# Planning the instruction order of a two-layer hybrid decoder with the framework's other timing model

## The chip, the core and the metric

The kernel runs on one core of one Trainium2 chip. The core has five engines that each work through a list of instructions of their own, in order: TensorE (PE, matrix products), VectorE (DVE), ScalarE (ACT), GpSimd (POOL) and SyncE (SP, which here only starts DMA transfers). They meet through semaphores. The metric is the device time of one execution in microseconds (us).

## What is computed

A prompt of 256 tokens and 8 samples of 4 tokens (T = 288 columns in all) go through two layers with shared weights. Layer 0 mixes tokens by retention (4 heads, chunked, rotary positions), layer 1 by a gated DeltaNet (GDN: short causal convolution, per-head decay, chunked delta rule). Each is followed by a gated ConvFFN with D_FF = 2816. Ahead of every sub-layer stands an RMS norm whose shift, scale and gate come from the conditioning vector c ("modulation"):

```python
for l in range(DEPTH):
    mod = cs @ p['w_ada'][l] + p['b_ada'][l]
    sh1, sc1, g1, sh2, sc2, g2 = jnp.split(mod, 6, axis=-1)
    h = ada_rmsnorm(x, p['norm_mix'][l], sh1, sc1)
    out, S = retention_mixer(h, ...) if l % N_MIXERS == 0 else gdn_mixer(h, ...)
    x = x + g1[:, None, :] * out
    h = ada_rmsnorm(x, p['norm_ffn'][l], sh2, sc2)
    out, buf = conv_ffn(h, s_fconv[l], p['w_ffn_up'][l], p['w_ffn_dw'][l], p['b_ffn_dw'][l], p['w_ffn_down'][l])
    x = x + g2[:, None, :] * out
y = ada_rmsnorm(x, p['norm_final'], shf, scf)
```

Outputs are y for both groups and the states that the mixers and convolutions leave. All is float32.

## The kernel before

The activations stay on the core; the weights, some 234 MB with the states, are streamed once. `plan_weights` lists them in the order of use as tiles of 128 x 1024 floats (512 KB), and `load` (L400) starts one DMA for each on SP's queue, into slots `raw` or `more` as these come free. A weight tile is split in two parts that a fast matmul can take, `whi` (a copy by ACT, L414) and `wlo` (the rest, by DVE, L415), and `product` (L533) makes 24 matmuls of it, each 128x128 by 128x288: eight each for `whi` with the high part of the activations (`hh`), `whi` with the low part (`hl`), and `wlo` with `hh`. The tiles' names tell the product: `pe`, `p`, `pv`, `pg` in retention, `fg` and `fv` up and `down` down in the ConvFFN, `gk`, `gv`, `gz` and `down` in GDN.

The modulation weights come as such tiles too. `ada_step` makes four matmuls of one, `adaP` (L453); eight tiles make a chunk, which ACT evicts (`adaev`) and `adaT` (L462) transposes. They wait for nothing but their DMA, and the source spreads them over the program, partly (`FILL`, `FILLS`, `ada_due`) at the places where a norm is made: ahead of its statistics `st_...` (L558), between these and their broadcast `rb_...` (L564, with DVE's inverse root between the two), and behind.

GDN works in four groups of four value heads. A group's work is a chain of small steps over PE, DVE and ACT: gates (`pg`), decays (`pd`, L1246), scores (`pa`, L1275; `pq`), an inverse by levels (`uc`, `pe` L1345), the heads' state chain (`pw`, `pn`, `po`), normalisation (DVE's `bigc`, L1618), the state update `gpS` (L1623), `px` (L1641) and `pxs` (L1647), then the gated output `gah` and the product `down`. The samples' states are loaded as tiles `gS` (L1436) and read by `pks` (L1466). `GDN_ORDER` and generators that `tick` steps inside the products (every six matmuls) interleave these chains with the large products in the source.

The order in which each engine gets its instructions is not the source order alone: the framework plans it from the source order and a timing model of its own, and the slots of a pool are given out by it too. `build` opens the pools and runs the stages; `__init__` calls it:

```python
with ExitStack() as ret:
    ...
    hs = self.retention(hs, lambda: self.h_split(1, 3, 4, "ffn0"))
hs = self.ffn(0, hs, 5, lambda: self.h_split(2, 6, 7, "gdn"))
hs = self.gdn(hs, lambda: self.h_split(3, 9, 10, "ffn1"))
self.ffn(1, hs, 11, self.finish)
```

Of the kernel before, what the change touches and what calls it, by code (L numbers as in the profile page):

```python
# [293 lines left out]
class Program:  # L294
    def __init__(self, ctx, tc, A, prm_offs, upto=99):
        self.ctx, self.tc, self.nc, self.A = ctx, tc, tc.nc, A
        self.upto = upto
        self.prm_offs = prm_offs
        self.cst_offs = shape_constants()[0]
        self.build()  # L300

    def pool(self, ctx, name, bufs=1, space=None):
        kw = {"space": space} if space else {}
# [1426 lines left out]
```

## Time and profile before

| what | value |
|---|---|
| median of 3 runs | 1236.14 us (1232.62 to 1408.05) |
| profiled execution, time | 1235.09 us |
| profiled execution, span from the first to the last instruction | 1233.3 us |
| PE busy | 1162.4 us (94%) |
| DVE busy | 877.2 us (71%) |
| ACT busy | 608.4 us (49%) |
| POOL busy | 326.0 us (26%) |
| DMA, mean over the span | 218 GB/s |
| granted TensorE clock, mean | 0.978 |

Busy time is the union of an engine's instructions. The stages follow one another on PE: retention up to about 345 us, the first ConvFFN to about 580, GDN to about 985, the second ConvFFN to about 1220, then the final norm.

### The profile page before, as it was taken

What the parts mean: (1) busy time and instruction counts of PE and PEld (TensorE: products, weight loads), DVE (VectorE), ACT (ScalarE), POOL (GpSimd) and SP (SyncE); (2) the same over time, 40 slices, a digit from 0 to 9 for tenths busy, and PEclk for the clock granted to TensorE, in tenths of its full rate; (3) what the DMA queues carried; (4) which work ended last, traced back from release to release, by engine and by line L of the source; (5) the groups of instructions that cost most, each with busy time, mean ns of one, the idle gap of its engine ahead of it and who ended that gap; (6) DMA issues with size and microseconds to landing.
All of it is one profiled execution on the core that took longest, in us unless ns stands there. A gap on an engine that the chain in (4) does not pass through costs nothing.

```text
span 1233.3 us, 24974 instructions
## 1 busy us (share of the span) xinstructions
PE 1162.4 (94%) x9486; PEld 1045.2 (85%) x9486; DVE 877.2 (71%) x2038; ACT 608.4 (49%) x1258; POOL 326.0 (26%) x504
## 2 busy tenths in 40 slices
PE   6999999999999999999889888988899899999996
PEld 2879788797969999997777777977789699999996
DVE  3657574765766666667769888797965687878785
ACT  2444534344446445543674655745544365555542
POOL 0214142151301221233242124243222212233241
PEclk9999999999999999999989998999999899999997
DMA  9999696866689556556636652534334997878521
GB/s 350 347 335 331 224 338 230 315 239 236 226 298 400 196 161 199 171 181 243 219 84 209 218 165 61 161 129 120 126 109 130 307 358 257 258 238 264 182 76 39
DMA packets 97480, 269.08 MB, mean 218 GB/s; under 512 B 26816, under 2 KB 28832, under 8 KB 97232
## 3 DMA queue, kind: packets, MB, share of 16 engines
q1 hardware_dynamic: 87456, 234.42, 56.6%
q0 software_dynamic: 8032, 29.16, 6.3%
q10 hardware_dynamic: 1872, 3.90, 0.9%
q8 instruction: 75, 1.23, 0.4%
q14 instruction: 45, 0.37, 0.1%
HBM read 236.06 MB, written 31.39 MB: 217 GB/s over the span
## 4 chain that ended last, share of the span: by engine, by line
PE 77%; DVE 13%; ACT 3%; DMA 3%; issue 2%; POOL 1%; ACTq 0%; POOLq 0%; DVEq 0%
PE down L533 17%; PE fg L533 12%; PE fv L533 11%; PE pg L533 4%; PE pv L533 4%; PE adaP L453 4%; PE p L533 3%; PE gv L533 2%; PE gz L533 2%; DVE mp L1319 2%; DVE wlo L415 2%; PE gk L533 2%; PE pO L884 1%; PE pU L903 1%; PE pS L854 1%
## 5 line engine op out<-in xcount | busy, mean ns | idle before, releaser
L415 DVE TENSOR_TENSOR wlo<-more,whi 128x1024 fp32r<-128x1024 f32 x138 | 171.1, 1241 | 80.6 <-ACT whi L414 67.8
L414 ACT CAST whi<-more 128x1024 fp32r<-128x1024 f32 x138 | 144.4, 1048 | 139.6 <-PE down L533 53.3
L414 ACT CAST whi<-raw 128x1024 fp32r<-128x1024 f32 x123 | 128.0, 1044 | 146.3 <-PE down L533 44.1
L415 DVE TENSOR_TENSOR wlo<-raw,whi 128x1024 fp32r<-128x1024 f32 x123 | 154.2, 1256 | 60.6 <-ACT whi L414 36.5
L702 POOL TENSOR_TENSOR x<-x,dt 128x32 f32<-128x32 f32 x159 | 103.1, 649 | 138.9 <-DVE dt L700 137.2
L698 DVE SCALAR_TENSOR_TENSOR x<-down,mod,x 128x256 f32<-128x256 f32 x160 | 76.7, 479 | 52.5 <-PE down L533 51.9
L580 POOL TENSOR_TENSOR fal<-cv,fah 128x288 fp32r<-128x288 f32 x44 | 41.2, 936 | 217.3 <-ACT fah L579 186.3
L533 PE MATMUL down<-fal,whi 128*128 128x288 f32 x352 | 64.5, 295 | 0.0
L533 PE MATMUL down<-fah,whi 128*128 128x288 f32 x352 | 62.2, 294 | 0.0
L533 PE MATMUL down<-fah,wlo 128*128 128x288 f32 x352 | 62.1, 294 | 0.0
L904 DVE SCALAR_TENSOR_TENSOR S<-S,pU 128x512 f32<-128x512 f32 x64 | 42.2, 684 | 24.5 <-PE pU L903 24.4
L533 PE MATMUL fg<-hh_ffn,whi 128*128 128x288 f32 x352 | 58.4, 298 | 0.8 <-ACT hh_ffn L626 0.7
L533 PE MATMUL fv<-hh_ffn,whi 128*128 128x288 f32 x352 | 58.7, 297 | 0.0
L533 PE MATMUL fg<-hh_ffn,wlo 128*128 128x288 f32 x352 | 55.0, 296 | 0.0
L533 PE MATMUL fv<-hh_ffn,wlo 128*128 128x288 f32 x352 | 54.7, 295 | 0.0
L533 PE MATMUL fv<-hl_ffn,whi 128*128 128x288 f32 x352 | 54.2, 295 | 0.0
L533 PEld LDWEIGHTS fg<-hh_ffn,whi 128*128 128x128 f32 x352 | 50.3, 188 | 4.6 <-ACT hh_ffn L632 2.2
L533 PE MATMUL fg<-hl_ffn,whi 128*128 128x288 f32 x352 | 54.0, 295 | 0.0
L533 PEld LDWEIGHTS down<-fal,whi 128*128 128x128 f32 x352 | 52.4, 188 | 0.4 <-issue 0.4
L533 PEld LDWEIGHTS down<-fah,whi 128*128 128x128 f32 x352 | 51.9, 188 | 0.8 <-ACT whi L414 0.8
L533 PEld LDWEIGHTS fv<-hh_ffn,whi 128*128 128x128 f32 x352 | 50.3, 188 | 2.5 <-ACT ftail L934 1.2
L533 PEld LDWEIGHTS down<-fah,wlo 128*128 128x128 f32 x352 | 51.9, 188 | 0.0
(467 smaller groups left out, 2921.3 us busy)
## 6 DMA issues: line engine op xcount, KB each, us to landing
more<-in_wu SPq DMA_DIRECT2D x73, 512.0 KB, 5.2
raw<-in_wada SPq DMA_DIRECT2D x69, 512.0 KB, 4.8
raw<-in_wgi SPq DMA_DIRECT2D x48, 512.0 KB, 3.9
more<-in_wada SPq DMA_DIRECT2D x43, 512.0 KB, 6.3
more<-in_wd SPq DMA_DIRECT2D x36, 512.0 KB, 3.8
S<-in_sr SPq DMA_DIRECT2D x16, 1024.0 KB, 8.5
out_rs<-S POOLq DMA_DIRECT2D x16, 1024.0 KB, 6.9
raw<-in_wri SPq DMA_DIRECT2D x28, 512.0 KB, 4.6
```

The lines of the kernel that those rows point to most:

```text
L414: nc.scalar.copy(hi[:, :c], r)
L415: nc.vector.tensor_tensor(lo[:, :c], r, hi[:, :c].bitcast(F32), ALU.subtract)
L453: nc.tensor.matmul(self.adaP[32 * g : 32 * g + 32, 0:256], lhsT=self.cs[:, k, :], rhs=rv[:, :, g, :], start=(k == 0), stop=(k == KT - 1), ...
L533: self.nc.tensor.matmul(out, lhsT=av[:, k, c0 : c0 + m], rhs=b[:, k, :], start=(k0 == 0 and i == 0), stop=(k1 == kts and i == len(seq) - 1))
L580: (nc.gpsimd if pool_lo else nc.vector).tensor_tensor(lo, src, hi.bitcast(F32), ALU.subtract)
L698: nc.vector.scalar_tensor_tensor(xm[:, :TP], p[:, :TP], g[:, 0:1], xm[:, :TP], ALU.mult, ALU.add)
L702: (nc.vector if gate == 11 and last and m == KT - 1 else nc.gpsimd).tensor_tensor(xv, xv, t, ALU.add)
L854: nc.tensor.matmul(pS, lhsT=kt[:, j, c * P : (c + 1) * P], rhs=vt[:, j, :], start=(j == 0), stop=(j == 1))
L884: nc.tensor.matmul(pO4[32 * g : 32 * g + 32, :], lhsT=qm[:, c, 4 * bb + g, :], rhs=S[bb, c][:, g, :], start=(bb == 0 and c == 0), stop=Fal ...
L903: nc.tensor.matmul(pU, lhsT=kms[g][:, c * P : (c + 1) * P], rhs=vst, start=True, stop=True)
L904: nc.vector.scalar_tensor_tensor(S[bb, c][:, g, :], S[bb, c][:, g, :], gamma4, pU, ALU.mult, ALU.add)
L1319: nc.vector.tensor_tensor(m, Ti[:, 0:k, :].rearrange("p j c -> p c j").unsqueeze(1).to_broadcast([P, w, 8, k]), X[:, 0:k, i:k].rearrange(" ...
```

## The change

The whole program is built inside a block of the framework that plans the order with its other timing model:

```diff
--- before.py
+++ after.py
@@ -297,7 +297,8 @@
         self.upto = upto
         self.prm_offs = prm_offs
         self.cst_offs = shape_constants()[0]
-        self.build()
+        with tc.block(schedule_with_timeline_sim=True), ExitStack() as self.ctx:
+            self.build()
 
     def pool(self, ctx, name, bufs=1, space=None):
         kw = {"space": space} if space else {}
```

The source order stays as it was, and every instruction is there as before; line numbers behind L300 and the numbers in names are one higher. The pools now close inside the block. What differs is the order on each engine, and with it the slots of the pools. The ConvFFN stages keep theirs; the three places below are in the other stages or between them.

First, SP's queue at the start, where tiles of retention weights (`in_wri`) and modulation weights (`in_wada`) are loaded. Before:

```order
L400 DMA raw<-in_wri 128x1024
L400 DMA raw<-in_wada 128x1024 x3
L400 DMA more_149<-in_wada 128x1024
L400 DMA raw<-in_wri 128x1024
L400 DMA more_161<-in_wada 128x1024
L400 DMA raw<-in_wada 128x1024
L400 DMA more_169<-in_wada 128x1024
L400 DMA more_197<-in_wada 128x1024
L400 DMA more_203<-in_wri 128x1024
L400 DMA more_205<-in_wri 128x1024
L400 DMA more_207<-in_wri 128x1024
L400 DMA more_209<-in_wri 128x1024
```

Now:

```order
L401 DMA raw<-in_wri 128x1024
L401 DMA raw<-in_wada 128x1024 x3
L401 DMA more_206<-in_wri 128x1024
L401 DMA more_150<-in_wada 128x1024
L401 DMA more_208<-in_wri 128x1024
L401 DMA more_210<-in_wri 128x1024
L401 DMA more_162<-in_wada 128x1024
L401 DMA more_170<-in_wada 128x1024
L401 DMA more_198<-in_wada 128x1024
L401 DMA more_204<-in_wri 128x1024
L401 DMA raw<-in_wri 128x1024
L401 DMA raw<-in_wada 128x1024 x3
```

The three `more` tiles of `in_wri` from the end of the first list have come forward between the modulation tiles, and the second `raw` tile of `in_wri` has gone from behind one modulation tile (`more_149`) to behind all of these.

Second, PE at the entry of the first ConvFFN: the last modulation matmuls ahead of the norm's statistics `st_ffn`, then its broadcast `rb_ffn`, then the first up products `fg` and `fv`. Before:

```order
L453 MATMUL adaP<-more_3435,c 32x256 x2
L453 MATMUL adaP<-more_3492,c 32x256 x4
L453 MATMUL adaP<-more_3631,c 32x256 x4
L453 MATMUL adaP<-raw,c 32x256 x5
L558 MATMUL st_ffn_3804<-ones,ssum 128x1 x3
L453 MATMUL adaP<-raw,c 32x256 x11
L462 MATMUL adaT<-cst,adaev 128x128 x2
L453 MATMUL adaP<-more_3786,c 32x256 x4
L564 MATMUL rb_ffn_3865<-cst,tr_ffn_3808 128x128 x2
L564 MATMUL rb_ffn_3865<-cst,tr_ffn_3808 128x32
L453 MATMUL adaP<-more_3792,c 32x256 x4
L533 MATMUL fg_3981<-hh_ffn_3769,whi 128x288
```

Now:

```order
L454 MATMUL adaP<-raw,c 32x256 x12
L454 MATMUL adaP<-more_3787,c 32x256 x4
L454 MATMUL adaP<-more_3793,c 32x256 x4
L454 MATMUL adaP<-more_3799,c 32x256 x4
L454 MATMUL adaP<-raw,c 32x256 x4
L559 MATMUL st_ffn_3805<-ones,ssum 128x1 x3
L463 MATMUL adaT<-cst,adaev 128x128 x2
L454 MATMUL adaP<-raw,c 32x256 x12
L565 MATMUL rb_ffn_3866<-cst,tr_ffn_3809 128x128 x2
L565 MATMUL rb_ffn_3866<-cst,tr_ffn_3809 128x32
L454 MATMUL adaP<-more_3856,c 32x256 x4
L534 MATMUL fg_3982<-hh_ffn_3770,whi 128x288 x3
```

Ahead of `st_ffn` there are now 28 matmuls `adaP` in a row where there were 15, behind it fewer, and three k-tiles of `fg` come in one go.

Third, PE at the end of GDN: the last `po` of group 3, its `gpS`, `px` and `pxs`, and the product `down` of its output (with `gah_11546` before, `gah_11547` now). Before:

```order
L1584 MATMUL po_11237<-bigc,gat_9611 128x128
L1586 MATMUL po_11237<-bigc,gat_9611 128x128
L533 MATMUL down<-gal_11050,whi 128x288 x2
L533 MATMUL down<-gah_11049,wlo 128x288 x4
...
L533 MATMUL down<-gal_11050,whi 128x288 x3
L1623 MATMUL gpS_11301<-bigc,kn_9444 128x256 x4
L533 MATMUL down<-gal_11050,whi 128x288
...
L533 MATMUL gz_11504<-hh_gdn,wlo 128x288 x8
L1641 MATMUL px_11530<-cst,bigc 128x128 x4
L1641 MATMUL px_11536<-cst,bigc 128x128 x4
L453 MATMUL adaP<-raw,c 32x256 x8
L1647 MATMUL pxs_11542<-cst,ons_11309 128x128
```

Now:

```order
L1585 MATMUL po_11238<-bigc,gat_9612 128x128
L1587 MATMUL po_11238<-bigc,gat_9612 128x128
L1585 MATMUL po_11238<-bigc,gat_9612 128x128
L1587 MATMUL po_11238<-bigc,gat_9612 128x128
L454 MATMUL adaP<-raw,c 32x256 x8
L1624 MATMUL gpS_11302<-bigc,kn_9445 128x256 x4
L1642 MATMUL px_11531<-cst,bigc 128x128 x4
L454 MATMUL adaP<-raw,c 32x256 x4
L1642 MATMUL px_11537<-cst,bigc 128x128 x4
L1648 MATMUL pxs_11543<-cst,ons_11310 128x128
L534 MATMUL down<-gah_11547,whi 128x288 x4
```

The `down` matmuls of group 2 and the products `gz` of group 3 that stood between `po`, `gpS` and `px` stand further up, ahead of this chain; between `po` and `gpS` there are eight matmuls `adaP` left.

## Rows read from the trace of the kernel before

**Rows 1.** Stages: stretch, length, busy PE, PEld, DVE, ACT, POOL (counts), clock, DMA, GB/s

```profile
0.00:50.00 50.00, 35.88 (x251) 22.37 (x252) 24.18 (x61) 16.29 (x29) 4.49 (x13) 0.97 0.92 354
50.00:345.00 295.00, 294.83 (x2191) 253.30 (x2190) 187.45 (x338) 130.77 (x226) 85.08 (x106) 1.00 0.77 275
345.00:600.00 255.00, 249.84 (x2035) 232.71 (x2036) 166.91 (x360) 121.46 (x219) 58.04 (x77) 1.00 0.69 236
600.00:900.00 300.00, 265.60 (x2456) 234.60 (x2455) 255.01 (x700) 172.95 (x465) 94.27 (x183) 0.95 0.46 140
900.00:990.00 90.00, 84.10 (x735) 74.37 (x734) 57.85 (x140) 40.70 (x86) 20.64 (x35) 0.96 0.62 198
990.00:1220.00 230.00, 229.15 (x1814) 225.10 (x1813) 180.12 (x426) 122.76 (x228) 63.50 (x91) 0.99 0.64 213
```

**Rows 2.** Waits of PE: waiter, releaser, total us, times, longest

```profile
PE pa L1275 <- DVE gat L1282: 6.9, 3, 2.9
...
PE pks L1466 <- DMA gS<-in_sg: 5.9, 6, 2.0
...
PE gpS L1623 <- DVE bigc L1618: 4.5, 3, 2.5
...
PE psy L1480 <- DVE t L1482: 2.3, 2, 2.2
...
PE gk L533 <- DVE gcv L1098: 1.8, 1, 1.8
...
PE pd L1246 <- ACT gat L1254: 1.0, 1, 1.0
...
PE pd L1246 <- POOL decay L1232: 0.8, 1, 0.8
```

**Rows 3.** Timeline of PE, first layer's start: start us, us, engine, line, operation

```profile
31.43 0.69 PE L533 MATMUL pe<-hh_ret,whi 128*128 128x288 f32 x4
31.95 0.69 PE L533 MATMUL pe<-hl_ret,whi 128*128 128x288 f32 x4
```

**Rows 4.** Timeline of SP's queue at the start; page's DMA issues, costliest groups

```profile
14.46 0.33 SPq L400 DMA_DIRECT2D more<-in_wada  x1
...
23.19 0.33 SPq L400 DMA_DIRECT2D raw<-in_wri  x1
...
raw<-in_wri SPq DMA_DIRECT2D x28, 512.0 KB, 4.6
...
L414 ACT CAST whi<-raw 128x1024 fp32r<-128x1024 f32 x123 | 128.0, 1044 | 146.3 <-PE down L533 44.1
```

**Rows 5.** Timeline of PE at the entry of the first ConvFFN

```profile
345.49 0.83 PE L558 MATMUL st_ffn<-ones,ssum 128*128 128x1 f32 x6 [0.56 <-DVE ssum L599]
...
351.81 0.40 PE L533 MATMUL fg<-hh_ffn,whi 128*128 128x288 f32 x1 [0.73 <-ACT hh_ffn L626]
...
353.57 0.64 PE L453 MATMUL adaP<-raw,c 128*32 128x256 f32 x8
```

**Rows 6.** One stretch there, columns as in the first group

```profile
348.00:352.00 4.00, 2.62 (x25) 1.45 (x26) 2.54 (x10) 1.27 (x4) 0.16 (x1) 1.00 1.01 398
```

**Rows 7.** Tile gS: its DMA to landing

```profile
DMA to landing us min/median/max: 3.8/4.6/6.3
```

**Rows 8.** Timeline of PE at the end of the GDN stage

```profile
931.03 0.39 PE L1586 MATMUL po<-bigc,gat 128*128 128x128 f32 x2
...
938.63 1.97 PE L1623 MATMUL gpS<-bigc,kn 128*128 128x256 f32 x8
...
955.48 1.04 PE L1641 MATMUL px<-cst,bigc 128*128 128x128 f32 x8
...
959.31 1.11 PE L533 MATMUL down<-gah,whi 128*128 128x288 f32 x6 [1.14 <-ACT gah L579]
```

**Rows 9.** Timeline of DVE at the same place

```profile
935.27 1.22 DVE L415 TENSOR_TENSOR wlo<-raw,whi 128x1024 fp32r<-128x1024 f32 x1
```

**Rows 10.** One stretch behind a gap in GDN, columns as in the first group

```profile
632.00:636.00 4.00, 4.00 (x14) 3.28 (x13) 2.80 (x10) 0.64 (x2) 0.71 (x1) 0.50 0.00 0
```

## Prediction

> **What bounds the kernel now.** I read first the busy time by stage, to see where TensorE (PE) can gain at all. In the retention stage, 50 to 345 us, PE is busy 294.83 of 295 us; in the second ConvFFN, 990 to 1220, 229.15 of 230, and in the stretch with the first ConvFFN 249.84 of 255 [rows 1]. There an order can lose time, not win any. The idle time lies in four places: the first 50 us (14.1 us, with the DMA engines at 0.92), the hand-over to the first ConvFFN around 345, the gated DeltaNet (GDN) stage from 600 to 900 (34.4 us idle, granted clock 0.95) with its end up to 990 (5.9 us) [rows 1], and the final norm behind 1220, after which no work is left that could be moved there.
>
> Next I read the waits of PE, to see what it stands on in GDN: DVE results (`pa` 6.9 us, `gpS` 4.5, `psy` 2.3, `gk` 1.8), state tiles still on their way (`pks` 5.9) and the decay tiles for `pd` (1.0 and 0.8) [rows 2]. DVE is itself busy for 255 of those 300 us [rows 1]: the chains belong to an engine with 45 us to spare, so more matmuls in a gap help only until DVE is the limit.
>
> **What the change does to the order.** No instruction is added or removed; each engine has the same list in another order. Counted in matmuls, the two ConvFFN stages keep their order. I matched the rows of both orders by tile and asked, for each moved matmul, what stands ahead of it now and how long that took before. Four matmuls of a product take 0.52 us (31.43 to 31.95 [rows 3]), one 0.13; one tile of modulation weights, `adaP`, four matmuls, takes 0.6 (0.64 with the last one's drain [rows 5]), one 0.15.
>
> Start. SP loads the second retention block seven tiles later than before (order, first place). A 512 KB tile takes 1.3 us at the 398 GB/s of a saturated stretch [rows 6], so seven are 9.2 us. But the queue stood still from 14.8 to 23.19 us, waiting for the slot of just this block [rows 4], and the seven loads go into other slots and can fill part of that pause. I take the block 6 us late (ends 0 and 9.2). Issued at 23.19 and landing in about 4.6 us, then split by a copy of 1.04 [rows 4], it was ready near 28.8; 6 later is 34.8, and its product ran at 31.43 [rows 3]. So the products that follow come about 3.4 us later; 12 matmuls of the fourth product, 1.6 us, are done ahead and come back. **+2 us** (0 to +6).
>
> Retention. PE has no idle to fill [rows 1]. Some products change places and the state updates come later; weights land well ahead. Two tiles of `adaP` stand 200 matmuls earlier than before, which can cost a landing. **+1** (0 to +4).
>
> Entry of the first ConvFFN (order, second place). The norm's statistics `st_ffn` have 27 more matmuls ahead of them, all `adaP`; the first `fg` has 24 more, six tiles or 3.6 us. In this stretch the DMA engines are full (share 1.01) and a tile lands each 1.3 us [rows 6], so PE consumes tiles twice as fast as they come; one whose slot is freed only six matmuls ahead must wait. I add 2.5 us for it, about two landings: `st_ffn` at about 352 instead of 345.49, first `fg` at about 358 instead of 351.81 [rows 5]. What returns is five tiles that stood between the `fg` rows (353.57 is one [rows 5]), 3 us. So 3.6 + 2.5 - 3: **+3** (0 if the tiles land ahead, +8 if each of the six waits out a landing, 6 x 1.3).
>
> Entry of GDN. `st_gdn` has 15 more `adaP` matmuls ahead, 2.3 us, of which most comes back since the rows behind it also hold them. **+1** (0 to +3).
>
> GDN, 600 to 900. Gains: where a waiting matmul now has 20 to 157 more matmuls ahead (2.7 to 20 us of work), its gap is covered: two of the three `pa` (6.9 less 1.8), the longest `gpS` 2.5, `psy` 2.2, `gk` 1.8, both `pd` 1.8, together 13.4 us [rows 2]. Losses: at the output of group 1 and the scores of group 2, PE would come up to 4.0 us ahead of DVE's result; at the next `gpS` 2.8; and the reload of one state tile has matmuls worth 2.0 us between the release of its slot and its reader, while such a load takes 4.6 us [rows 7]: 2.6. Together 9.4. **-4** (-13 if all gains hold and the losses are absorbed, +8 if DVE's chain sets the pace and only the losses show).
>
> End of GDN, 900 to 990 (order, third place). Before, 49 `down` matmuls of group 2 stand between the last `po` (931.03) and `gpS` (938.63), and 17 more with four `gz` products between `gpS` and `px` (955.48); the normalising chain from `po` to `gpS`, 7.2 us (931.4 to 938.63), ran under the 49 [rows 8]. Now these fillers come ahead of group 3's chain, and only two `adaP` tiles (1.2 us) stand between `po` and `gpS`. The old chain shared DVE with a weight split of 1.22 us and updates of the residual [rows 9]; without these I put it at 5.5, so 4.3 us lie open. From `px` to the first `down` it is 3.8 us as before (955.48 to 959.31, with its 1.14 of idle), and 0.6 us more as less stands in it [rows 8]. **+5** (+3 to +9: the whole chain and a stretch of half clock).
>
> On the clock: from 632 to 636 us, just behind a gap, the granted clock is 0.50, the 1.2 GHz level, with PE at work all the time [rows 10]; that stretch cost 2 us. The Trainium skill, "TensorE: Matmul & The Clock Gate", section "What's actually happening", says that the halved clock is the resting state and activity lifts it. The trace agrees. By that rule the open wait at the end of GDN would cost these 2 us on top, and the sum would be 1245; I leave it out, because the gaps that are filled in GDN would give as much back.
>
> Second ConvFFN and final norm: **0**.
>
> Sum: 2 + 1 + 3 + 1 - 4 + 5 = 8 us. The profiled execution took 1235.09 us, 1.05 below the median of the runs shown; 1235.1 + 8 gives **1243 us**.
>
> **Rivals.** *No change:* the same work, PE bound for 780 us in an order that stays, and the moved tiles land in time because the queue also issues them earlier. For it: full PE in three stages [rows 1]. Against it: at the end of GDN the cover is visibly gone. 1235 us.
>
> *Faster:* the planner fills GDN. If two thirds of its 34.4 idle us go (23) and half of what the clock of 0.95 costs over 300 us (7.5), while the rest costs 8, it gives 1235 - 23 - 7.5 + 8 = 1213 us. It decides from the point where DVE's idle falls from 45 us to some 15; against it stands that each chain must then run with hardly a gap.
>
> *Slower, by loads:* `adaP` tiles stand ahead of the norms' statistics at all three hand-overs, and an in-order PE waits there for landings, with everything behind. Six tiles at the first ConvFFN, four at GDN, and as many at the second ConvFFN, 14 x 1.3 = 18 us, with the upper ends of start (+6) and end of GDN (+9) and no gain in GDN (+3): 1271 us. It decides if a tile's landing moves less than its use, on the queue's pace of 1.3 us per tile [rows 6]. Against it: SP's slots also come free earlier when the tiles before them are used earlier.
>
> **How the numbers follow.** Forecast 0.50 (its own range 1235 to 1253), no change 0.18, faster 0.12, slower by loads 0.20. The range that leaves out 2 in 10 reaches into both sides: 1223 to 1268. By 2%, 24.7 us, about what a measurement of this kernel can tell from no change, the bounds are 1211 and 1261: half of the faster case lies below the first (0.06), most of the slower case above the second (0.17); the rest, 0.77, within.
>
> **What would show it.** Right: `po` to `gpS` of group 3 with a PE wait of 4 to 5 us; first `fg` near 358; PE idle in GDN from 34 to about 30 and DVE still near 85%; ConvFFN stretches as long as before. Wrong: a wait of `adaP` on DMA above 10 us in total (slower), PE idle in GDN below 20 us (faster), or the second retention block landing as early as before (start costs nothing).

## The result, and the profile after

The kernel became slower: 1308.33 us, the median of 4 runs (1299.46 to 1312.57), against 1236.14 before. The ratio is 1.0597 with an interval of 1.0568 to 1.0627; it leaves out slow runs, such as the 1408.05 us of the kernel before. The forecast was 1243 with a range up to 1268; the time lies outside it, on the side of the rival *slower, by loads*, and beyond that rival's 1271 too.

The head of the page after, and its row of the granted clock (40 slices, in tenths; an 8 or 7 is a slice with half clock in it):

```profile
span 1309.9 us, 24985 instructions
PE 1199.3 (92%) x9486; PEld 1073.0 (82%) x9486; DVE 883.6 (67%) x2038; ACT 607.5 (46%) x1258; POOL 323.9 (25%) x504
PEclk8899989999989999999879998899998789999998
```

PE's 9486 matmuls are the same, yet its busy time went from 1162.4 to 1199.3 us (+36.9), and its idle time from 1233.3 - 1162.4 = 70.9 to 110.6 (+39.7). So the loss has two halves: PE waits longer, and it works slower. The mean granted clock fell from 0.978 to 0.942. With levels of 1 and 0.5, that is 2 x 0.022 of the span (54 us) at the half clock before, and 2 x 0.058 (152 us) after. Summed over the stretches at the half clock, PE is busy for 40.0 us before and for 114.7 after. The same work takes about twice as long there (four matmuls of `pe` 1.33 us for 0.69), so about half of the 74.7 us more, 37.3, is what the slow clock added: the whole rise of the busy time. DVE, ACT and POOL are as busy as before.

By stage, with the stretches cut at the same places of the program as in [rows 1]; columns are stretch, length, busy PE, PEld, DVE, ACT, POOL, clock, DMA share, GB/s:

```profile
0.00:58.00 58.00, 36.72 (x256) 24.75 (x256) 22.56 (x57) 16.15 (x29) 1.95 (x10) 0.82 0.86 333
58.00:373.00 315.00, 303.43 (x2176) 257.51 (x2176) 185.63 (x332) 128.47 (x225) 77.07 (x106) 0.98 0.72 257
373.00:637.00 264.00, 252.84 (x2007) 233.55 (x2007) 167.83 (x358) 117.95 (x213) 57.04 (x78) 0.96 0.66 217
637.00:961.00 324.00, 286.06 (x2533) 253.50 (x2532) 256.57 (x698) 179.92 (x475) 97.48 (x179) 0.92 0.45 135
961.00:1068.00 107.00, 89.56 (x698) 78.36 (x697) 65.73 (x156) 38.99 (x84) 24.14 (x41) 0.86 0.61 206
1068.00:1298.00 230.00, 228.78 (x1819) 223.69 (x1817) 179.59 (x421) 122.46 (x227) 66.21 (x91) 1.00 0.60 194
```

Against [rows 1]: 50, 295, 255, 300 and 90 us became 58, 315, 264, 324 and 107; only the second ConvFFN keeps its 230 (the stretch of the first holds its entry and that of GDN too). The retention stage, which had 0.2 us of PE idle, now has 11.6.

The matmuls of a stretch are not quite the same ones in both kernels. A finer measure is the **lag**: the start of the n-th matmul after, less the start of the n-th before, counted over the 9486 matmuls that both traces have. What it grew by in each part of the program, beside the terms of the forecast:

| part (time in the kernel before) | forecast | lag at its end | growth |
|---|---|---|---|
| start, to 52 us | +2 | 6.4 | +6.4 |
| retention, to 345 | +1 | 28.6 | +22.2 |
| entry of the first ConvFFN, to 369 | +3 | 36.0 | +7.4 |
| first ConvFFN, to 580 | 0 | 37.0 | +1.0 |
| entry of GDN, to 600 | +1 | 42.6 | +5.6 |
| GDN, to 905 | -4 | 55.8 | +13.2 |
| end of GDN, to 990 | +5 | 77.8 | +22.0 |
| second ConvFFN, to 1200 | 0 | 78.8 | +1.0 |

The order also moves work across these borders, so a few us between neighbours mean little: at 52 us the lag is 6.4 with the modulation matmuls counted and 10.5 without them (the expectations below say 8), and inside GDN it stands at 61.4 at 800 us. The two GDN rows together are +35.2 where I had +1.

The waits of PE after (waiter, releaser, total us, times, longest):

```profile
PE adaP L454 <- DMA raw<-in_wada: 9.2, 7, 4.1
...
PE pe L1346 <- DVE uc L1335: 7.9, 4, 4.3
PE pd L1247 <- POOL decay L1233: 6.3, 2, 5.1
PE pe L534 <- ACT whi L415: 5.1, 1, 5.1
...
PE adaP L454 <- DMA more<-in_wada: 4.5, 5, 1.9
PE gz L534 <- DVE gcv L1099: 3.7, 1, 3.7
...
PE pso L1490 <- ACT t L1485: 3.2, 1, 3.2
...
PE gpS L1624 <- DVE bigc L1619: 2.3, 3, 1.1
PE pU L904 <- DVE S L905: 2.2, 10, 0.5
...
PE pks L1467 <- DMA gS<-in_sg: 1.7, 1, 1.7
```

Against [rows 2], most gains arrived: `pa` (6.9) is all but gone, `pks` on its DMA fell from 5.9 to 1.7 (a new wait of 1.9 for DVE's `t` beside it), `gpS` from 4.5 to 2.3. But waits that hardly existed before took their place: `pe` for DVE's `uc`, `pd` for POOL's `decay` (0.8 in [rows 2], now 6.3), `gz`, `pso`; and `adaP` on its DMA grew from 3.5 to 13.7.

### The profile page after: what moved, and what is told of

Its sections match the earlier page's. It is cut to its first block, busy times and chain, and to the rows that moved or that the text cites. A ratio compares the mean times of both kernels' runs of the same rounds, so it can differ in the third digit from the quotient of the medians.

```text
span 1309.9 us, 24985 instructions
## 1 busy us (share of the span) xinstructions
PE 1199.3 (92%) x9486; PEld 1073.0 (82%) x9486; DVE 883.6 (67%) x2038; ACT 607.5 (46%) x1258; POOL 323.9 (25%) x504
## 4 chain that ended last, share of the span: by engine, by line
PE 70%; DVE 13%; DMA 9%; ACT 3%; issue 2%; POOL 1%; SPq 1%; DVEq 0%; ACTq 0%; POOLq 0%
PE down L534 16%; PE fv L534 11%; PE fg L534 11%; PE pg L534 4%; PE adaP L454 4%; PE pv L534 4%; PE p L534 3%; PE gz L534 3%; PE gv L534 2%; DVE wlo L416 2%; DMA more<-in_wada 2%; DVE mp L1320 2%; PE pO L885 1%; DMA raw<-in_wada 1%; DVE Ti L1324 1%
## 5 line engine op out<-in xcount | busy, mean ns | idle before, releaser
L703 POOL TENSOR_TENSOR x<-x,dt 128x32 f32<-128x32 f32 x159 | 99.5, 628 | 145.4 <-DVE dt L701 140.7
L905 DVE SCALAR_TENSOR_TENSOR S<-S,pU 128x512 f32<-128x512 f32 x64 | 42.6, 682 | 25.2 <-PE pU L904 25.1
L454 PE MATMUL adaP<-raw,c 128*32 128x256 f32 x552 | 49.0, 417 | 9.2 <-DMA raw<-in_wada 9.2
L1320 DVE TENSOR_TENSOR mp<-Ti,X 128x48 f32<-128x48 f32 (+7 forms) x64 | 46.9, 733 | 8.6 <-POOL X L1313 7.9
```

The costliest lines, as they stand in the source:

```text
L454: nc.tensor.matmul(self.adaP[32 * g : 32 * g + 32, 0:256], lhsT=self.cs[:, k, :], rhs=rv[:, :, g, :], start=(k == 0), stop=(k == KT - 1), ...
L703: (nc.vector if gate == 11 and last and m == KT - 1 else nc.gpsimd).tensor_tensor(xv, xv, t, ALU.add)
L905: nc.vector.scalar_tensor_tensor(S[bb, c][:, g, :], S[bb, c][:, g, :], gamma4, pU, ALU.mult, ALU.add)
L1320: nc.vector.tensor_tensor(m, Ti[:, 0:k, :].rearrange("p j c -> p c j").unsqueeze(1).to_broadcast([P, w, 8, k]), X[:, 0:k, i:k].rearrange(" ...
```

## The experiments

Every kernel below is the kernel **before**, with its instructions issued in an order that I write down; three kinds add some instructions too. The edit that pins the order is the same each time, only the table differs:

```diff
-        self.build()
+        self.build(); pin(tc)
...
+    for steps in json.loads(zlib.decompress(base64.b64decode(ORDER))):
+        n, last = 0, None
+        for s in steps:
+            n += s
+            if last:
+                tc.add_manual_dep(by[f"I-{n}"], last, info, reason="pin")
+            last = f"I-{n}"
```

`pin` says for each engine which instruction follows which, and adds no wait between engines. The table itself costs nothing that can be seen: `warm` below, pinned to the order of before, takes as long as the kernel before.

**Is it the order, or the block?** The first theory is that the order alone makes the loss; the rival, that the block does (pools that close earlier, other semaphores). The table of `order_only` is the whole order of after:

> The kernel before, without the block, with each engine pinned to the order that the changed kernel has. If the order alone makes the loss (theory order): about 1308 us, with half clock for some 150 us in all as in the changed kernel. If the block itself costs (theory block: its pools close inside, slots are given out another way): near 1236 us, and the loss stays unexplained by any row order.

Measured: 1306.92 us against 1233.24, ratio 1.0601 (1.054 to 1.0662). The order alone gives the whole loss, with 130 us of half clock in its trace, and the rival falls.

**Which stretch?** Five tables take after's order for a stretch of the program and before's for the rest. `start_only`, up to 48 us:

> The kernel before, with the changed kernel's order only for what the kernel before starts in its first 48 us. Theory local (each stretch of the new order costs by itself what the two traces show at its end): +8 us, 1244. Theory carried (a stretch costs little by itself, and what is late at its end makes the next ones lose): +2 as in my sum, 1238.

`retention_only`, 48 to 345 us:

> The kernel before, with the changed kernel's order only for what the kernel before starts between 48 and 345 us. Theory local: +20 us (the lag grows from 8 to 28 us in this stretch of the two traces), 1256, with new half-clock stretches at the runs of state updates. Theory carried: +1 to +4 as in my sum, 1237 to 1240.

`entry_only`, 300 to 400 us (so the last head of retention is in it, and in the run above as well):

> The kernel before, with the changed kernel's order only for what the kernel before starts between 300 and 400 us: the end of retention and the entry of the first ConvFFN. Theory local: +12 us (lag from 22 to 36, less what belongs to the last head's updates), 1248, with a half-clock stretch at the first up products. Theory carried: +3 as in my sum, 1239.

`gdn_middle_only`, 580 to 905 us:

> The kernel before, with the changed kernel's order only for what the kernel before starts between 580 and 905 us. Theory local: +18 us (lag 37 to 55 in the two traces), 1252, with about as many new half-clock stretches as in the changed kernel there (nine, against five before). Theory carried: -4 as in my sum, 1230.

`gdn_end_only`, from 905 us on:

> The kernel before, with the changed kernel's order only for what the kernel before starts after 905 us. Theory local: +20 us (lag 55 to 78 in the two traces), 1254, from the open chain of group 3, waits of adaP for DMA and the half clock behind them. Theory carried: +5 as in my sum, 1238.

| run (number of runs) | median, us | before, us | ratio and interval | loss, us |
|---|---|---|---|---|
| start_only (6) | 1241.83 | 1233.24 | 1.0064 (1.0032 to 1.0097) | 8.6 |
| retention_only (2) | 1266.78 | 1233.24 | 1.0275 (1.0182 to 1.0369) | 33.5 |
| entry_only (2) | 1245.28 | 1233.24 | 1.0101 (1.0048 to 1.0153) | 12.0 |
| gdn_middle_only (2) | 1269.00 | 1234.14 | 1.0272 (1.0167 to 1.0377) | 34.9 |
| gdn_end_only (7) | 1245.60 | 1234.14 | 1.0091 (1.0054 to 1.0127) | 11.5 |

Every stretch loses by itself, so the losses arise in the stretches and are not only carried in from the one before; the two that I had at +1 and -4 lose the most. The sum, 100 us, is more than the 74 of the whole order, as a cut has a price of its own: in `retention_only` an `adaP` waits 6.66 us right behind the cut, for a tile whose load stayed at its old place, and 8 us of lag arise there; in `gdn_middle_only` 6 arise at the cut at 905. So the two large runs bound their stretches from above, and the growth of the lag in the table before is the better size. `gdn_end_only` loses 11.5 where the lag had grown by 22. That lag jumps by 16 between 905 and 916 us, right at the cut, and falls back by 8 up to 956, so what the end of GDN costs by itself is open between the two.

**What loses time in retention?** The timeline of after, second head, shows one cause (start, us, engine, line, operation, count, and in brackets the idle time ahead and its releaser):

```profile
170.73 0.73 PE L904 MATMUL pU<-vst,km 128*128 128x512 f32 x2
172.10 1.07 PE L904 MATMUL pU<-vst,km 128*128 128x512 f32 x2 [0.64 <-DVE rsu_ret L549]
173.35 0.49 PE L904 MATMUL pU<-vst,km 128*128 128x512 f32 x1 [0.18 <-DVE S L905]
174.03 0.50 PE L904 MATMUL pU<-vst,km 128*128 128x512 f32 x1 [0.18 <-DVE S L905]
...
177.15 3.76 PE L855 MATMUL pS<-vt,kt 128*128 128x512 f32 x4
179.93 1.95 PE L534 MATMUL down<-ah,whi 128*128 128x288 f32 x4
...
182.30 0.69 PE L534 MATMUL down<-ah,wlo 128*128 128x288 f32 x4
```

A state update is a chain: each `pU` on PE is followed by an addition to the state `S` on DVE, which must empty the buffer before a later `pU` may fill it. The page of before has its price, 0.68 us each:

```profile
L904 DVE SCALAR_TENSOR_TENSOR S<-S,pU 128x512 f32<-128x512 f32 x64 | 42.2, 684 | 24.5 <-PE pU L903 24.4
```

Before, two `pU` at most stood next to each other, with other matmuls between the pairs. Now runs of 5, 8, 6 and 5 stand together, and PE goes through them at DVE's pace, one each 0.7 us. Behind the run the clock is at half:

```profile
176.00:180.00 4.00, 4.00 (x12) 2.43 (x10) 3.27 (x6) 0.00 (x0) 0.75 (x1) 0.50 0.94 378
```

The first four matmuls of `down` take 1.95 us there (the first of them starts while the last `pS` still runs), where four of the same product take 0.69 a little later.

The runs are not the whole loss of this stage. Of its 11.6 us of idle time 4.3 stand ahead of a `pU`; 3.6 are `adaP` waiting for a landing and 2.3 `down` waiting for DVE's `dt`, and neither was tried by itself.

`bunched` makes such runs in before's order and leaves the rest as it was. It moves five `pU` together, and six that then stand ahead of a seventh, and DVE's additions along with them:

```diff
-L903 MATMUL pU_1531<-vst_1395,km_1444 128x512
-L533 MATMUL pg_1582<-hl_ret,whi 128x288 x3
-L903 MATMUL pU_1597<-vst_1395,km_1539 128x512
...
 L838 MATMUL pO_1630<-cst_r,o_1561 128x32
+L903 MATMUL pU_1531<-vst_1395,km_1444 128x512
+L903 MATMUL pU_1597<-vst_1395,km_1539 128x512
+L903 MATMUL pU_1572<-vst_1395,km_1537 128x512
```

> The kernel before in its own order, but in the retention stage five state-update matmuls pU of head 0 and six of head 1 stand in a run, each at the place of the last of them, and DVE's updates S that read them too (the changed kernel has runs of 5, 8, 6 and 5; the kernel before none over 2). Theory run (PE goes at DVE's pace of 0.68 us for each pU, as two PSUM buffers alternate, and comes back at half clock): +2.5 to 5 us at each of the two runs, 5 to 10 in all, 1239 to 1244. Theory loads (the loss in retention is from weight and modulation tiles that land late): no change, 1234.

Measured: 1242.36 us against 1233.97, ratio 1.007 (1.0047 to 1.0094), 8.4 us for two runs of updates moved by a few places, as the theory *run* had it. Timeline of PE at the second run:

```profile
155.94 3.71 PE L903 MATMUL pU<-vst,km 128*128 128x512 f32 x5 [2.05 <-DVE S L904]
159.45 1.64 PE L533 MATMUL pg<-hh_ret,wlo 128*128 128x288 f32 x6
```

and its stretches, columns as above:

```profile
152.00:156.00 4.00, 1.95 (x14) 1.46 (x12) 1.17 (x3) 2.31 (x6) 0.00 (x0) 1.00 0.74 282
156.00:160.00 4.00, 3.87 (x8) 2.03 (x9) 3.54 (x6) 0.34 (x2) 1.51 (x2) 0.55 0.63 261
160.00:164.00 4.00, 4.00 (x19) 3.73 (x19) 2.81 (x5) 1.12 (x3) 0.19 (x1) 0.60 0.90 308
```

In the middle stretch PE does eight matmuls, at a clock of 0.55, and the next stretch is slow for the most part as well (0.60). The lag grows by 6.3 us here and by 2.0 at the run of 5. The longest wait here, 2.05 us, is not the pace of the links. DVE stood still ahead of the first of the moved additions, as an addition `oss` that waits for ScalarE stands in front of it in DVE's list:

```profile
154.83 0.46 DVE L843 TENSOR_TENSOR oss<-oss,osq 128x288 f32<-128x288 f32 x1 [4.24 <-ACT osq L841]
155.20 1.96 DVE L904 SCALAR_TENSOR_TENSOR S<-S,pU 128x512 f32<-128x512 f32 x3
```

So a run of chain links, on both engines of the chain, is a cause and can be shown apart from the rest of the new order; up to 2 of the 6.3 us come from where its links stand on DVE.

**The same in GDN.** `gdn_first` takes after's order between 602 and 660 us only. There `pd` sums of one group (each fed by `decay` tiles of POOL and `gat` of ACT) stand next to each other, because the `gv` product between them has gone ahead:

```diff
-L533 MATMUL gv_7170<-hl_gdn,whi 128x288 x6
-L533 MATMUL gv_7170<-hh_gdn,wlo 128x288 x8
-L1275 MATMUL pa_7279<-kqT_6862 128x512
 L1246 MATMUL pd_7122<-decay_7073,after_r 128x256 x2
...
-L1164 MATMUL pq_7138<-ones,t1m_7101 128x1 x2
 L1246 MATMUL pd_7177<-decay_7130,after_r 128x256 x2
```

> The kernel before, with the changed kernel's order only for what the kernel before starts between 602 and 660 us: the first group of GDN, where the new order puts five sums of decays (pd) next to one another on PE. Theory run (PE goes at the pace of the chain decay on GpSimd, pd, exponential on ScalarE, some 2.6 us a step, with half clock behind it): +7 to +12 us, 1241 to 1246, with PE waits of 1 to 5 us at each pd. Theory spread (the loss in GDN is made by many small waits of the later groups): within 3 us of 1234.

Measured: 1243.39 us against 1230.57, ratio 1.0098 (1.0063 to 1.0133), a loss of 12.8. Its timeline of PE:

```profile
634.30 0.80 PE L1246 MATMUL pd<-decay,after_r 128*128 128x256 f32 x2 [5.05 <-POOL decay L1232]
...
636.88 0.80 PE L1246 MATMUL pd<-decay,after_r 128*128 128x256 f32 x2 [1.25 <-POOL decay L1232]
...
639.72 0.77 PE L1246 MATMUL pd<-decay,after_r 128*128 128x256 f32 x2 [0.98 <-ACT gat L1256]
...
643.16 0.76 PE L1246 MATMUL pd<-decay,after_r 128*128 128x256 f32 x2 [2.13 <-ACT gat L1254]
```

and the stretch that holds them:

```profile
634.00:648.00 14.00, 9.03 (x38) 6.55 (x42) 4.03 (x15) 5.48 (x11) 5.58 (x9) 0.51 0.00 1
```

The four waits, 9.4 us, are those of after at the same place (5.05, 1.25, 0.98 and 2.13), and the clock stays at 0.51 from the end of the first of them to the end of the last. Other matmuls move in this stretch too; the run of `pd` without them was not tried.

**What does the clock add?** `waits` leaves the order of before and adds four waits of growing length to the first ConvFFN, where PE has none: a chain of 1, 4, 8 and 14 copies on ScalarE (0.398 us each) behind a small matmul, and a matmul that waits for it. `waits_filled_2` gives PE 10, 22 and 40 matmuls that nobody reads to do in the last three:

```diff
+    nc.tensor.matmul(g[:, 0:1], lhsT=self.ones, rhs=self.ones[:, 0:1], start=True, stop=True)
...
+    for i in range(FILL_N.get(m, 0)):
+        nc.tensor.matmul(d[:, 0:288], lhsT=hs[0][:, i % KT, 0:P], rhs=hs[0][:, i % KT, :], start=True, stop=True)
...
+    nc.scalar.copy(t, g[:, 0:1].to_broadcast([P, 288]))
+    for i in range(GAP[m] - 1):
+        nc.scalar.copy(t, t)
+    nc.tensor.matmul(g[:, 1:2], lhsT=t[:, 0:P], rhs=self.ones[:, 0:1], start=True, stop=True)
```

> The kernel before in its own order, with four waits put into the first ConvFFN where PE else never stops: a small matmul, a chain of 1, 4, 8 and 14 copies of 288 columns on ScalarE, and a small matmul that waits for the chain (about 0.8, 2, 3.8 and 6.5 us). Theory clock (a wait costs more than itself, as TensorE comes back at half clock): behind the longer ones a half-clock stretch, and the lag against the kernel before grows by the wait and 1.5 to 3.5 us more; some 18 us in all. Theory plain (a wait costs its length): the lag grows by the waits alone, 13 us.

> The same four waits, with 10, 22 and 40 matmuls of 128x128 by 128x288 whose results nobody reads put into the last three. Theory clock: no half clock in the first ConvFFN, and the lag grows by the waits alone, 13 us in all: 3 to 7 less than with empty waits. Theory plain: the same time as with empty waits.

> The four added waits again, with 10, 22 and 40 unread matmuls in the last three, now into a PSUM tile of their own, so that the chain on ScalarE does not wait for them. Theory clock: no half clock in the first ConvFFN, the lag grows there by the waits alone, 11 to 13 us in all against 18 to 19 with empty waits. Theory plain: the same lag as with empty waits.

The first filled kernel, `waits_filled` (1266.72 us), says nothing: its filling matmuls wrote the same tile that the chain reads, so ScalarE waited for them. The two others ran once each, 1251.69 and 1246.95 us. The two longest waits, in `waits` (PE's timeline, then the stretch behind each):

```profile
476.65 0.59 PE L1750 MATMUL gap<-ones,gap_t 128*128 128x1 f32 x2 [3.73 <-ACT gap_t L1749]
...
531.56 0.59 PE L1750 MATMUL gap<-ones,gap_t 128*128 128x1 f32 x2 [6.50 <-ACT gap_t L1749]
```

```profile
474.00:484.00 10.00, 7.35 (x45) 6.60 (x46) 1.90 (x4) 4.99 (x12) 0.79 (x1) 0.66 0.19 52
529.00:541.00 12.00, 9.44 (x56) 9.44 (x57) 3.21 (x7) 6.30 (x14) 0.80 (x1) 0.72 0.08 25
```

The same places in `waits_filled_2`:

```profile
474.00:484.00 10.00, 9.32 (x78) 8.34 (x77) 2.79 (x6) 5.76 (x14) 0.80 (x1) 1.00 0.38 117
527.00:539.00 12.00, 10.95 (x83) 10.70 (x81) 4.38 (x8) 7.15 (x15) 1.56 (x2) 1.00 0.22 52
```

The program is held up equally long at both places in both kernels (from 472.64 to 476.65 us and from 472.45 to 476.47, for the first), but the clock stays at 1.00 where PE has something to do. At the same matmuls of the program the lag grew by 6.5 and 9.3 us in `waits`, by 4.2 and 7.2 in `waits_filled_2`: the half clock adds 2.3 us to a wait of 3.73, and 2.1 to one of 6.50, so about 2 us to either. The two short waits (0.49 and 1.88 us) were followed by no half clock.

`warm` tries whether that can be won back in the kernel before: 68 unread matmuls ahead of five of its waits in GDN (`pa`, `pks`, `gpS`).

```diff
+WARM = {('pa', 0): ('c', 18), ('pa', 2): ('c', 10), ('pa', 3): ('b', 13), ('gpS', 2): ('e', 15), ('pks', 3): ('a', 12)}
...
+                warm(self, 'pa', g)
```

> The kernel before in its own order, with 68 unread matmuls of 128x128 by 128x288 in five groups ahead of matmuls of the GDN stage that wait 1.8 to 2.9 us (three pa, one pks, one gpS). Theory clock: the half-clock stretches near 630, 770, 842 and 893 us (20 us together) go or shorten, and the kernel gains 3 to 8 us: 1226 to 1231. Theory plain: the added matmuls fit into the waits and nothing changes, 1234, or it is slower by their overhang.

Measured: 1232.69 us against 1233.97, ratio 0.9992 (0.9973 to 1.0011): no difference. In its trace the half clock behind three of the waits is gone (that near 630 us is still there) and the lag is -2.5 us at the end; a gain of that size can't be told from none here, and no version beat the kernel before.

**The end of GDN, and the start.** After's timeline of PE at the end of GDN:

```profile
1020.46 0.39 PE L1587 MATMUL po<-bigc,gat 128*128 128x128 f32 x2
1020.78 0.64 PE L454 MATMUL adaP<-raw,c 128*32 128x256 f32 x8
1025.49 1.08 PE L454 MATMUL adaP<-raw,c 128*32 128x256 f32 x8 [4.07 <-DMA raw<-in_wada]
1026.50 3.78 PE L1624 MATMUL gpS<-bigc,kn 128*128 128x256 f32 x8
```

The wait is where I put it, between `po` and `gpS`, but it is `adaP` that waits, for a landing. Is the load the cause, or does it only cover the chain? `gdn_end_ada_back` is `gdn_end_only` with the modulation tiles back behind the chain:

```diff
 L1586 MATMUL po_11237<-bigc,gat_9611 128x128
-L453 MATMUL adaP<-raw,c 32x256 x8
 L1623 MATMUL gpS_11301<-bigc,kn_9444 128x256 x4
```

> As the run with only the end of GDN in the new order, but the modulation tiles of that stretch (adaP, adaT, their eviction and their loads) at the places of the kernel before, so that nothing stands between the last po and gpS. Theory chain (my step: the normalising chain lies open): PE waits 5 us for bigc ahead of gpS and the time stays near 1245. Theory landing (PE waits there for a modulation tile that is loaded too late): the 4 us wait is gone, and the time falls to 1237 to 1240.

Measured: 1251.01 us against 1233.97, ratio 1.0145 (1.0109 to 1.0181), not better than 1.0091 with the tiles there, and 6 us above the theory *chain*, for a reason that stays open. Its timeline of PE, at the chain and at the hand-over to the ConvFFN:

```profile
961.66 3.46 PE L1623 MATMUL gpS<-bigc,kn 128*128 128x256 f32 x8 [5.52 <-DVE bigc L1618]
...
989.04 1.08 PE L453 MATMUL adaP<-raw,c 128*32 128x256 f32 x8 [2.33 <-DMA raw<-in_wada]
```

The chain takes the 5.5 us that the forecast gave it, with nothing to cover it. From the start of the last `po` to `gpS` it is 5.9 us here and 6.0 in after with the tiles between. The load was a stand-in, not the cause.

At the start, after waits 5.12 us for the split `whi` of the second retention block (the 5.1 among the waits above). `start_loads` is `start_only` with the loads on SP back in before's order:

```diff
-L400 DMA more_205<-in_wri 128x1024
 L400 DMA more_149<-in_wada 128x1024
-L400 DMA more_207<-in_wri 128x1024
-L400 DMA more_209<-in_wri 128x1024
+L400 DMA raw<-in_wri 128x1024
 L400 DMA more_161<-in_wada 128x1024
```

> As the run with only the start in the new order (8.6 us slower), but with the loads on SP's queue in the order of the kernel before. Theory load (PE stands for the second retention block, loaded seven tiles later): its wait of 5 us and the half clock behind it go, and the time falls to 1234 to 1237. Theory matmuls (the modulation matmuls moved ahead delay the first norm and the second halves): it stays at 1240 to 1243.

Measured: 1244.11 us against 1230.57, ratio 1.0115 (1.0085 to 1.0145); nothing came back. ScalarE's timeline in this run:

```profile
34.65 1.04 ACT L414 CAST whi<-more 128x1024 fp32r<-128x1024 f32 x1 [8.85 <-DMA more<-in_wri]
...
38.16 1.04 ACT L414 CAST whi<-raw 128x1024 fp32r<-128x1024 f32 x1
```

The block (`raw`) now landed near 27 us, but ScalarE takes its splits in after's order, and three `more` tiles, whose loads went back, stand ahead of it. So SP's loads and ScalarE's splits are one order in two queues; this run turned one of them alone and shows no more than that. What the loads by themselves cost at the start stays open.

## Why the prediction was wrong, step by step

**Start, +2: right place, too small (+6.4, alone +8.6).** I had the block 6 us late and its product 3.4. In after's trace SP issued it at 24.67, only 1.5 us late, but it landed at 35.8, 11 us later, behind the loads that now stand in front of it: the time to landing that I had taken as fixed (4.6, [rows 4]) was what grew. ScalarE could split it 8.3 us late (35.84 for 27.53), near my upper end of 9.2, and its product began at 36.94 instead of 31.43 [rows 3]. I charged the wait and not the slow clock around it: it is at half from 25 to 42 us (before from 26 to 30), the stage's clock is 0.82 against 0.97 [rows 1], and four matmuls of `pe` take 1.33 us in place of 0.69. A further wait of 2.18 us, for `hh_ret` at 48.95, was not in the sum either.

**Retention, +1: the step that failed most (+22.2).** I read "PE has no idle to fill" [rows 1] as "little can happen here", and wrote that the state updates come later without asking what then stands next to them. The price was in the trace of before: a `pU` hands over to 0.68 us of DVE work, so six in a row take 4 us where they had been free between other matmuls. `bunched` shows two such runs at 8.4 us; after has four, and how the rest of the 22 divides was not tried.

**Entry of the first ConvFFN, +3: right mechanism, too small (+7.4).** After's timeline of PE there:

```profile
378.02 0.83 PE L559 MATMUL st_ffn<-ones,ssum 128*128 128x1 f32 x6
...
381.17 0.64 PE L454 MATMUL adaP<-raw,c 128*32 128x256 f32 x8 [1.21 <-DMA raw<-in_wada]
383.81 1.08 PE L454 MATMUL adaP<-raw,c 128*32 128x256 f32 x8 [2.00 <-DMA raw<-in_wada]
...
388.95 1.09 PE L534 MATMUL fg<-hh_ffn,whi 128*128 128x288 f32 x3 [1.63 <-ACT hh_ffn L627]
```

Without the lag of 28.6 us with which the stage begins, `st_ffn` stands at 349.4 (352 forecast, 345.49 before) and `fg` at 360.4 (358 forecast, 351.81 before). The tiles wait for two landings, 3.4 us with a short third, where I had 2.5, but between the statistics and their broadcast, so the norm's chain itself is late. And the 3 us that were to come back, came back to about one. The larger part of the miss is the clock, which the sum left out here: from 384 to 396 us it is 0.50 after, with PE busy for 9.78 of the 12 us, half of which is 4.9; before it stays at 1.00 through the whole stretch [rows 1].

```profile
384.00:396.00 12.00, 9.78 (x49) 7.21 (x46) 8.98 (x20) 5.13 (x11) 1.04 (x1) 0.50 0.91 296
```

**Entry of GDN, +1 (+5.6).** I moved matmuls past the statistics and priced them; the first products that wait for the norm's result (`pba`, 2.5 and 1.9 us of wait) were not in the sum.

**GDN, -4: half of it right (with its end, +35.2 for +1).** The gains of `pa` and `gpS` came and that of `psy` on DVE's `t` (2.3 to 0.7, though its wait for ACT's `t` went from 1.9 to 2.6), and the only wait for a state tile is 1.7 where I had 2.6 for a reload. But the two `pd` waits, which I counted as 1.8 us covered, became four of 9.4 together, and `gk` waits for other results as long as before. The error is in the method. I counted how many matmuls now stand ahead of a waiting one, and took the other engines' results to come when they came before. But the matmuls that were put ahead of one wait had stood between the links of another chain, and there the chain's own pace (POOL's `decay`, DVE's `uc`, ACT's `t`) became PE's. My upper end, +8 "if DVE's chain sets the pace", comes nearest, but it was made of other losses: the next `gpS`, for which it had 2.8, waits 1.1 at most.

**End of GDN, +5: place and wait right, the rest missing.** Forecast was a wait of 4 to 5 us between `po` and `gpS`; it is 4.07, and 5.52 with the tiles out of the way. From `px` to `down` it is 4.30 us (1030.07 to 1034.37, with 1.63 of wait for `gah`) where I had 3.8 and 0.6 more, so that part is right too. Missing were the clock (`gpS` takes 3.78 us in place of 1.97 [rows 8], and half clock stands again at 1035 to 1042 and at 1056 to 1065), and the hand-over to the second ConvFFN, where `st_ffn` waits 2.12 us for 0.92 before and `fg` 1.62 for none (two landings, 2.0 us before, are gone).

**The clock, left out.** I expected the filled gaps to give back what the open ones cost. The half clock went from some 54 to 152 us instead, and PE's busy time rose by 36.9. By the Trainium skill, "TensorE: Matmul & The Clock Gate", section "Terms", time at a throttled clock costs about the share that is missing, here half: 98 us more would be an estimated 49. The trace agrees only for the part in which PE was at work, 74.7 us, half of which is 37.3; for the rest of that time it was waiting. The clock, for which I named 2 us and took none, was worth half of the loss.

**Right.** Both ConvFFN stages keep their length (+1.0 and +1.0); the gains of `pa`, `gpS` and, beyond the forecast, `pks` came; DVE did not become the limit in GDN (79% busy).

**The rivals.** *Slower, by loads* had the right sign. `adaP` waits 13.7 us for DMA after, and 3.5 before: above the 10 us that I named as its mark. But that is 10.2 of 39.7 us of new idle time, and at the end of GDN the load only stood in front of a chain as long. The mark was met though loads are not the main cause, so it was a poor mark. The rest of the idle time is chains on DVE, POOL and ACT, a rival that I had not named. *Faster* falls: GDN's idle grew from 34.4 to 37.9 us. *No change* falls.

## What to carry to other kernels

When an order changes, look for links of one chain that come to stand next to each other on the waiting engine, and price each by the partner engine's time for a link; matmuls that cover a wait in their new place have uncovered another in their old one, so a stage with no idle time has much to lose (22 us in retention here). Count the slow clock behind each longer wait (about 2 us on top of one of 3.73 and of one of 6.50 here), and behind a run of links too: in this kernel it made half of the loss. Pinning the order of one stretch at a time finds the place, but a cut between two orders can cost some us of its own (6 and 8 at two of them here).

## What the runs showed of the hardware

The half clock does not stand behind single long waits alone. In after, at the run of eight `pU`, PE's longest idle time is 0.64 us, and the clock is at 0.50 from 176 to 180 us. In `bunched` PE's longest idle time at the run is 2.05 us, and the clock is at 0.55 in the stretch behind it, where PE does single matmuls at DVE's pace; it is at 0.60 in the next 4 us and was back at full speed only while the large products that follow were running. In `gdn_first` PE goes through 14 us of small sums and waits at 0.51. Two waits of 3.73 and 6.50 us cost about the same 2 us of slow clock on top. In `waits` a single wait of 1.88 us, with dense products on both sides, was followed by none.
